# RWKV-7 branch of a hybrid decoder layer: groups of four head pairs over 256 tokens instead of two over 512

## The chip, the cores and the metric

The kernel runs on one core of a Trainium2 chip. The core has TensorE (matmuls, called PE in the profile; PEld is its weight load), VectorE (DVE), ScalarE (ACT), GpSimd (POOL) and SyncE (SP), which here only issues transfers. The metric is device time in microseconds for one execution; less is better.

## The reference, cut to what matters

One layer, 2048 tokens, model width 1024, float32. A normalised input is projected into three branches; each branch's output is gated, projected back, merged and added to the input. Branch A is the one that changes:

```
p = rms_norm(x) @ w_in                       # split into p_r, p_k, p_v, p_w, p_a, z_a, ...
r, k, v = token_shift_mix(...)               # u + (prev - u) * mu
decay = exp(-exp(-softplus(-(w0 + tanh(lw) @ w2)) - 0.5))
a = sigmoid(a0 + la @ a2)
kk = k * k_k / max(norm(k * k_k), 1e-12);  k = k * (1 + (a - 1) * k_a)
step t, per head (64 x 64 state S):
    S = S * w_t + (S @ -kk_t) kk_t*a_t  + v_t k_t ;  y_t = S @ r_t
y = group_norm(y) * lnx_g + lnx_b + sum(r * k * r_k) * v
y_a = y * silu(z_a)
```

There are eight heads of 64 channels. Branch B is sliding-window attention, branch C cross-attention into 256 memory tokens.

## The kernel before, in words

The tokens are taken in four superblocks of 512 (TB). The channels lie on the partitions, tokens on the free axis. The kernel keeps float32 accuracy by writing each operand as a rounded part and a rest (type f32r), so that a product is three matmuls of 512 columns (gemm3, L467 to L469). Weights come from DRAM block by block: a block is 128 x 1024 (a `whl` tile, eight buffers), loaded by SP (L445), and feeds twelve matmuls. In the first superblock the rounded parts are made on chip (L449, L450) and kept in DRAM.

Per superblock two streams are woven together: stream_r, the RWKV branch, and stream_f, the other branches with their merges. The recurrence is done in chunks of 64 tokens (C). The eight heads are four pairs, a pair filling 128 partitions (heads EV and OD). Stream_r works on two groups of two pairs, each over all 512 tokens, that is eight chunks (NC_):

- rwkv_prep, once a pair: projections of k, r and v with the token shift; products for decay and rate (L702 to L706, 512 columns); the norm of k (tok_stat L509 in the first superblock, spread_sums L520 and L521 later); the tiles QE, QO, AB and BK of each chunk; the Gram products of BK with QE and QO (L769, 32 matmul records for each of two heads' halves in one burst); transposes of BK (L786) and v (L801); the bonus sums (L795, L796). The second pair's four tiles take four of the eight `whl` buffers until the group's chain ends.
- rwkv_inverse, once a group: the inverse of a triangular block per chunk, on VectorE (L819 to L821), with two bursts of 32 x 32 matmuls.
- rwkv_chain, once a group: a serial loop over the eight chunks. In a step TensorE computes pw from the state (L899), VectorE copies it (W, L903), TensorE pu (L914), VectorE multiplies it by the key norms into Z (L920), TensorE the new state pS (L923), and VectorE adds to it SP, the old state times the chunk-end decay Pl, with pS itself multiplied by Pl (L924, four operations a step). SP is made on ScalarE (L912, four a step). Two more bursts for the outputs y (L879, L875) don't hold the loop up. TensorE's rows for these small float32 matmuls come in two records each.

The order of the work is not the order of the code. Every instruction is recorded, and a list scheduler (lay_out) with a duration for each kind of instruction (cost_PE, cost_DVE and so on), a rank by place in the code and the free buffers of each pool writes one fixed order for each engine; then these orders are tied down. The numbers that the streams yield weave their code order. Each queue works strictly in that order: an instruction that waits holds everything behind it on its engine, and a transfer that waits for a buffer or its data holds the transfers behind it on SP.

Of the kernel before, what the change touches and what calls it, by code (L numbers as in the profile page):

```python
# [9 lines left out]
F32 = mybir.dt.float32  # L10
# [4 lines left out]
ALU = mybir.AluOpType  # L15
# [13 lines left out]
NC_ = TB // C  # L29
# [278 lines left out]
def build(tc, A, nsb=4):  # L308
# [114 lines left out]
    smask = bp.tile([128, TB], BF16, name="smask")  # L423
# [99 lines left out]
    def half_sums(d, out, junk):  # L523

        j = chunks(junk)
        V.tensor_tensor(j, chunks(out), eye64.unsqueeze(1).to_broadcast([128, NC_, 64]), op=ALU.mult)
        V.tensor_reduce(d, j, axis=AX.X, op=ALU.add)
# [138 lines left out]
    Pt = cp.tile([128, NC_, 65], F32, name="Pt")  # L666
    G.memset(Pt, 1.0)
# [14 lines left out]

    EV, OD = slice(0, 64), slice(64, 128)
# [3 lines left out]
    def rwkv_prep(p, i, Z, dk, Nc, sb, hT, lwla, group):  # L687
        def big(name):

            if not i:  # L690
                return rp.tile([128, NC_, 128], F32, name=name)
            t = wp.tile([128, NC_, 128], F32, name="whl")
            G.memset(t[:, 0, 0:1], 0.0)
            return t

        QE, QO, AB, BK = (big(n) for n in ("QE", "QO", "AB", "BK"))
        bk = BK.rearrange("p c (s t) -> p c s t", t=C)
        kp = proj(B_K + p, hT)
        k = shift(kp, B_K + p, pcol("mu_k", p), dcol("omu_k", p), sb, "rk_")
        lh, ll = (t.rearrange("p (a c) -> p a c", a=4) for t in wblock(A["w2a2"][p], ("lora", p)))  # L700
        pw = rw_ps()
        PE.matmul(pw, lh[:, 0], lwla[0], start=True, stop=False)  # L702
        PE.matmul(pw, ll[:, 2], lwla[0], start=False, stop=True)
        pa = rw_ps()
        PE.matmul(pa, lh[:, 1], lwla[1], start=True, stop=False)
        PE.matmul(pa, ll[:, 3], lwla[1], start=False, stop=True)  # L706
        th = tmp()
        S.activation(th, pw, AF.Tanh, scale=0.5, bias=dcol("hw0", p))
        ta = tmp()
        S.activation(ta, pa, AF.Tanh, scale=0.5, bias=dcol("ha0", p))  # L710
        V.tensor_scalar(th, th, 1.0, None, op0=ALU.add)
        cum = tmp()
        V.tensor_tensor_scan(cum, smask, th, 0.0, ALU.mult, ALU.add)
        S.activation(Pt[:, :, 1:], chunks(cum), AF.Exp, scale=-DEC)
        Pl = xp.tile([128, NC_], F32, name="Pl", bufs=4)
        S.activation(Pl, Pt[:, :, C], AF.Copy)
        iP = tmp()
# [4 lines left out]
        yield 10.317  # L722
        st = rw_ps()
        if sb >= FIRST:
            sq = tmp()
            S.activation(sq, k, AF.Square, scale=pcol("k_k", p))
            spread_sums(st, ones2, sq, *(rp.tile([128, TB], F32R, name="rt", bufs=NRT) for _ in range(2)))
            half_sums(dk[:, i], st, sq)
            V.tensor_scalar(dk[:, i], dk[:, i], 1e-24, None, op0=ALU.max)
        else:  # L730
            sq = tmp()
            S.activation(sq, k, AF.Square, scale=pcol("k_k", p))
            tok_stat(sq, 2, 4, st)
            sums, own = st[:, :8].rearrange("p (a e) -> p a e", e=2), dk[:, i].rearrange("p (a o) -> p a o", o=2)
            for e, h in ((0, EV), (1, OD)):
                for o, at in ((0, EV), (1, OD)):
                    V.tensor_scalar(own[h, :, o], sums[at, :, e], 1e-24, None, op0=ALU.max)
# [3 lines left out]
        kkh = tmp()  # L741
# [3 lines left out]
        t2 = tmp()  # L745
# [3 lines left out]
        f = tmp()  # L749
# [5 lines left out]
        rpj = proj(B_R + p, hT)  # L755
        r = shift(rpj, B_R + p, pcol("mu_r", p), dcol("omu_r", p), sb, "rr_")
# [4 lines left out]
        yield 12  # L761

        two = ((QE, EV, OD), (QO, OD, EV))
        gs, ms = [], []
        for c0 in range(0, NC_, 4):
            gs.append([t.rearrange("p (c t) -> p c t", c=4) for t in ((rw_ps(), rw_ps()) if not c0 else (y_ps(), o_ps()))])
            for c in range(4):
                for (Q, h, oh), g in reversed(list(zip(two, gs[-1]))):
                    m = PE.matmul(g[:, c], BK[h, c0 + c], Q[h, c0 + c], start=True, stop=True)  # L769
                    if ms:  # L770
                        behind(m, ms[-1])
# [11 lines left out]
        for c0 in range(0, NC_, 4):  # L783
            pk = rw_ps().rearrange("p (c f) -> p c f", c=4)
            for c in range(4):
                PE.transpose(pk[:, c], BK[:, c0 + c], ident)  # L786
# [642 lines left out]
```

## Time and profile before

| | before |
|---|---|
| runs | 2232.64 us median of 3 (2232.46 to 2233.23) |
| the profiled execution, its span | 2231.6 us |
| TensorE | 2210.5 us busy, 13682 matmul records |
| VectorE | 1544.4 us busy, 3993 instructions |
| ScalarE | 920.2 us busy, 2042 instructions |
| GpSimd | 132.9 us busy |
| transfers | 433.17 MB, mean 194 GB/s |

The profiled execution's first to last instruction, 2231.6 us, is 1.0 us under the median. Busy time counts an engine as busy from the start to the end of each instruction; matmuls overlap, so the distances between their starts tell more than their durations. A group's line gives busy time and the mean duration of one, then the engine's idle time before it and what ended it.

### The profile page before, as it was taken

The numbers are of one execution on the slowest core, as the hardware profiler recorded it, in microseconds if no ns is written. First come the engines' busy times: TensorE is split into PE (matmuls) and PEld (weight loads), VectorE is DVE, ScalarE is ACT, GpSimd is POOL, SyncE is SP. The second block draws the span as 40 slices with busy tenths as digits, with TensorE's granted clock in tenths as the row PEclk, the third lists the DMA queues.
The fourth block names the chain that finished last, engine by engine and source line by source line (L and its number), as shares of the span: only waits on it lengthen the run. The fifth ranks groups of instructions, "written<-read, shape, count | busy, mean of one in ns | idle before, by whom it ended". The sixth has DMA issues, their size and how long they took to land. (4 is left out here: it accounts for less than half of the span.)

```text
span 2231.6 us, 36859 instructions
## 1 busy us (share of the span) xinstructions
PE 2210.5 (99%) x13682; PEld 1798.2 (81%) x13682; DVE 1544.4 (69%) x3993; ACT 920.2 (41%) x2042; POOL 132.9 (6%) x193
## 2 busy tenths in 40 slices
PE   8999999999999999999999999999999999999999
PEld 7888778778888778878888878877888887887887
DVE  7799699775479688943438958975245896896312
ACT  6664565445253355423215335432223434534210
POOL 1000010000000010000000001000000001000000
PEclk9999999999999999999999999999999999999999
DMA  6877556679845434446764534445675444344555
GB/s 218 293 240 258 186 183 217 224 274 351 313 163 167 143 133 158 146 169 231 243 237 143 178 125 150 144 142 199 222 254 198 162 156 156 119 151 132 201 196 189
DMA packets 149874, 433.17 MB, mean 194 GB/s; under 512 B 16704, under 2 KB 24256, under 8 KB 149696
## 3 DMA queue, kind: packets, MB, share of 16 engines
q1 hardware_dynamic: 133568, 401.45, 53.0%
q10 hardware_dynamic: 16128, 29.37, 3.9%
q8 instruction: 109, 1.79, 0.3%
q14 instruction: 69, 0.57, 0.1%
HBM read 334.81 MB, written 95.94 MB: 193 GB/s over the span
## 5 line engine op out<-in xcount | busy, mean ns | idle before, releaser
L467 PE MATMUL mm<-hH,whl 128*128 128x512 f32 x1888 | 752.4, 399 | 0.1
L469 PE MATMUL mm<-hH,whl 128*128 128x512 f32 x1888 | 750.2, 397 | 0.0
L468 PE MATMUL mm<-hL,whl 128*128 128x512 f32 x1888 | 745.3, 395 | 0.0
L469 PEld LDWEIGHTS mm<-hH,whl 128*128 128x128 f32 x1888 | 355.1, 188 | 71.8 <-issue 1.5
L467 PEld LDWEIGHTS mm<-hH,whl 128*128 128x128 f32 x1888 | 355.3, 188 | 68.7 <-DVE carry L677 0.4
L468 PEld LDWEIGHTS mm<-hL,whl 128*128 128x128 f32 x1888 | 355.3, 188 | 68.0 <-issue 0.9
L449 ACT ACTIVATE whl<-raw 128x512 fp32r<-128x512 f32 x178 | 111.3, 629 | 151.3 <-PE mm L469 95.1
L450 DVE TENSOR_TENSOR whl<-raw,whl 128x512 fp32r<-128x512 f32 x178 | 122.5, 691 | 48.2 <-ACT whl L449 45.9
L467 PE MATMUL mm<-yh,whl 128*128 128x512 f32 x384 | 151.9, 396 | 1.3 <-ACT gt L1190 0.8
L468 PE MATMUL mm<-yl,whl 128*128 128x512 f32 x384 | 151.1, 393 | 0.0
L469 PE MATMUL mm<-yh,whl 128*128 128x512 f32 x384 | 150.2, 391 | 0.0
L912 ACT ACTIVATE SP<-Z,Pl 64x64 f32<-64x64 f32 x256 | 76.4, 337 | 117.1 <-DVE Z L924 115.5
L819 DVE STREAM_SHUFFLE ibc<-Nc 128x496 f32<-128x496 f32 (+30 forms) x248 | 114.0, 473 | 0.0
L1205 DVE SCALAR_TENSOR_TENSOR g<-g,mm 128x512 f32<-128x512 f32 x32 | 21.8, 682 | 128.3 <-PE mm L469 128.3
L820 DVE TENSOR_TENSOR ibc<-ibc,Yi 128x496 f32<-128x496 f32 (+30 forms) x248 | 104.9, 423 | 4.1
L821 DVE TENSOR_TENSOR Yi<-Yi,ibc 128x496 f32<-128x496 f32 (+30 forms) x248 | 103.5, 418 | 1.2
L924 DVE SCALAR_TENSOR_TENSOR Z<-rw,Pl,SP 64x64 f32<-64x64 f32 x224 | 63.4, 283 | 40.6 <-PE rw L923 37.1
L1190 ACT ACTIVATE gt<-mm 128x512 f32<-128x512 f32 x64 | 37.9, 592 | 118.3 <-PE mm L469 118.2
L467 PEld LDWEIGHTS mm<-yh,whl 128*128 128x128 f32 x384 | 72.2, 188 | 16.9 <-ACT gt L1190 1.2
L468 PEld LDWEIGHTS mm<-yl,whl 128*128 128x128 f32 x384 | 72.2, 188 | 14.6
L1152 ACT ACTIVATE g<-g,mxs,st 128x256 f32<-128x256 f32 (+1 forms) x128 | 74.5, 584 | 22.8 <-DVE mxs L1145 22.6
L469 PEld LDWEIGHTS mm<-yh,whl 128*128 128x128 f32 x384 | 72.2, 188 | 14.4
(1847 smaller groups left out, 3804.7 us busy)
## 6 DMA issues: line engine op xcount, KB each, us to landing
whl<-k SPq DMA_DIRECT2D x486, 512.0 KB, 3.3
k<-whl SPq DMA_DIRECT2D x162, 512.0 KB, 4.3
raw<-in_w_in SPq DMA_DIRECT2D x118, 256.0 KB, 3.2
g<-in_x ACTq DMA_DIRECT2D x32, 256.0 KB, 4.9
out<-g ACTq DMA_DIRECT2D x32, 256.0 KB, 4.3
raw<-in_w_proj SPq DMA_DIRECT2D x24, 256.0 KB, 3.1
rt<-in_x ACTq DMA_DIRECT2D x24, 256.0 KB, 5.2
rt<-in_xt ACTq DMA_DIRECT2D x24, 256.0 KB, 5.5
```

Source lines behind the costliest of these rows:

```text
L449: S.activation(w[:, 0], raw, AF.Copy)
L450: V.tensor_tensor(w[:, 1], raw, w[:, 0].bitcast(F32), op=ALU.subtract)
L467: PE.matmul(out, lh, rh, start=i == 0, stop=False)
L468: PE.matmul(out, lh, rl, start=False, stop=False)
L469: PE.matmul(out, ll, rh, start=False, stop=i == n - 1)
L819: V.stream_shuffle(bc[:, :, :w], N_[:, :, s + 1:], [s] * 32)
L820: V.tensor_tensor(bc[:, :, :w], bc[:, :, :w], Y[:, :, s:s + 1].to_broadcast([128, n, w]), op=ALU.mult)
L821: V.tensor_tensor(Y[:, :, s + 1:], Y[:, :, s + 1:], bc[:, :, :w], op=ALU.add)
L912: S.activation(SP[h, i], Z[h, i, e, c], AF.Copy, scale=g[4][h, c:c + 1])
L924: upds = [V.scalar_tensor_tensor(Sst[h, g[0]] if c == NC_ - 1 else Z[h, i, e, c + 1], pS[h, i, e], g[4][h, c:c + 1], SP[h, i], op0=ALU.mul ...
L1152: S.activation(prs[b][:, i, m0:], prs[b][:, i, m0:], AF.Exp, scale=r2[:, b, i:i + 1], bias=mx[:, b, i:i + 1], accum_out=mx[:, b, 2 + i:3 + i])
L1190: S.activation(t, gp, AF.Tanh, scale=0.5)
```

## The change

A group is now all four pairs over half a superblock (TR = 256 tokens, so four chunks), and the halves follow each other. What a group holds is as large as before; the loop is four steps long with four pairs in each, where it was eight steps with two.

- Projections of k, r and v are still made once for 512 tokens, in the first half's rwkv_prep. The second half of each result (128 x 256) is stored to DRAM by SP and loaded again when the second half's rwkv_prep wants it (columns). The gate z_a is made in the second half.
- The other operations of rwkv_prep and the end of rwkv_chain work on 256 columns and run twice as often. The low-rank weights are loaded once for each half. The first superblock uses spread_sums, too.
- BK is multiplied by Pl (a new VectorE operation a pair and half, 128 x 512) after its Gram products and before its transposes. So pS comes out multiplied, and the step's update is an addition for all pairs of a head side: two VectorE operations. SP is made by two VectorE operations for all pairs, not by four ScalarE ones.
- The first two pairs' tiles come from a pool with two buffers, those of the last two pairs from four `whl` buffers. Pt has two tiles.

```diff
+TR = 256
+NC_ = TR // C
...
+    def bigs(i):
+        if i < 2:
+            return [rp.tile([128, NC_, 128], F32, name=n, bufs=2) for n in ("QE", "QO", "AB", "BK")]
+        out = []
+        for _ in range(2):
+            t = wp.tile([128, 2, NC_, 128], F32, name="whl")
...
+    def columns(what, p, half, sb, make, tile):
+        if half:
+            t = tile[:, :TR]
+            nc.sync.dma_start(t, later_half.pop((what, p)))
             return t
+        t = make(tile)
+        d = later_half[what, p] = dp.tile([128, TR], F32, name=f"{what}{sb}_{p}")
+        nc.sync.dma_start(d, t[:, TR:])
+        return t[:, :TR]
...
-        k = shift(kp, B_K + p, pcol("mu_k", p), dcol("omu_k", p), sb, "rk_")
+        k = columns("k", p, half, sb, lambda t: shift(proj(B_K + p, hT), ...), rp.tile([128, TB], F32, name="rk_"))
-        PE.matmul(pw, lh[:, 0], lwla[0], start=True, stop=False)
+        PE.matmul(pw, lh[:, 0], lwla[0][:, cut], start=True, stop=False)
...
+        V.tensor_tensor(BK, BK, Pl[:, i].unsqueeze(2).to_broadcast([128, NC_, 128]), op=ALU.mult)
+        pk = rw_ps().rearrange("p (c f) -> p c f", c=NC_)
...
-            for i, e, h, g in HH:
-                S.activation(SP[h, i], Z[h, i, e, c], AF.Copy, scale=g[4][h, c:c + 1])
+            for e, h in ((0, EV), (1, OD)):
+                V.tensor_tensor(SP[h], Z[h, :n, e, c], Pl[h, :n, c:c + 1].to_broadcast([64, n, C]), op=ALU.mult)
...
-            upds = [V.scalar_tensor_tensor(... pS[h, i, e], g[4][h, c:c + 1], SP[h, i], op0=ALU.mult, op1=ALU.add)
-                    for i, e, h, g in HH]
+            upds = [V.tensor_tensor(Sst[h, :n] if c == NC_ - 1 else Z[h, :n, e, c + 1], pS[h, :, e], SP[h], op=ALU.add)
+                    for e, h in ((0, EV), (1, OD))]
...
-            for p0 in range(0, 4, n):
+            for half in range(TB // TR):
...
+                for p in range(4):
+                    yield from rwkv_prep(p, Z, dk, Pl, Nc, sb, half, hT, lwla, group, yas)
```

The program's order around three places of the prediction. First TensorE, part of one step of the chain in the last superblock. Rows of 128x512 are other work; rw<-Z is pw, yps is y, rw<-W is pu, rw<-Z of 128x128 is pS. Before:

```order
L899 MATMUL rw<-Z,QE 64x64
L899 MATMUL rw<-Z,QO 64x64
L899 MATMUL rw<-Z,whl 64x64 x2
L879 MATMUL yps<-Z,QE 64x64
L879 MATMUL yps<-Z,QO 64x64
L879 MATMUL yps<-Z,whl 64x64 x2
L467 MATMUL mm<-hH,whl 128x512
L468 MATMUL mm<-hL,whl 128x512
L914 MATMUL rw<-W,AB 64x64 x2
L914 MATMUL rw<-W,whl 64x64 x2
L875 MATMUL yps<-Z,AB 64x64 x2
L875 MATMUL yps<-Z,whl 64x64 x2
```

The same place in the changed program (L910 is the old L899, L890 and L886 the old L879 and L875, L925 the old L914):

```order
L910 MATMUL rw<-Z,whl 64x64 x4
L890 MATMUL yps<-Z,QE 64x64
L890 MATMUL yps<-Z,QO 64x64
L890 MATMUL yps<-Z,QE 64x64
L890 MATMUL yps<-Z,QO 64x64
L890 MATMUL yps<-Z,whl 64x64 x4
L469 MATMUL mm<-hL,whl 128x512
L925 MATMUL rw<-W,AB 64x64 x4
L925 MATMUL rw<-W,whl 64x64 x4
L886 MATMUL yps<-Z,AB 64x64 x4
L886 MATMUL yps<-Z,whl 64x64 x4
L470 MATMUL mm<-hH,whl 128x512
```

Each burst has twice the matmuls of before, and one 512-column matmul stands between y and pu where there were two.

Second VectorE, the loop's operations. Before (rows of 128x512 are a merge of the other stream):

```order
L1205 SCALAR_TENSOR_TENSOR gt<-gt,mm 128x512
L1206 TENSOR_TENSOR mB<-mB,gt 128x512
L903 COPY W<-rw 128x128
L920 TENSOR_TENSOR Z<-rw,dk 64x2x64 x2
L924 SCALAR_TENSOR_TENSOR Z<-rw,Pl,SP 64x64 x4
L903 COPY W<-rw 128x128
```

And in the changed program (L914 copies W, L931 makes Z, L935 updates, L923 makes SP):

```order
L849 COPY ibc<-rw 32x512 x2
L914 COPY W<-rw 128x256
L931 TENSOR_TENSOR Z<-rw,dk 64x4x64 x2
L935 TENSOR_TENSOR Z<-rw,SP 64x4x64 x2
L923 TENSOR_TENSOR SP<-Z,Pl 64x256 x2
L914 COPY W<-rw 128x256
```

The update is two operations instead of four, and SP's two stand behind it, ahead of the next copy of W. (ibc belongs to the inverse.)

Third SP's queue while a group is prepared in the last superblock. Before, only weight blocks stand there:

```order
L445 DMA whl<-k_3789 128x1024
L445 DMA whl<-k_3797 128x1024
L445 DMA whl<-k_3804 128x1024
L445 DMA whl<-k_3938 128x1024
L445 DMA whl<-k_3946 128x1024
L445 DMA whl<-k_3953 128x1024
```

In the changed program's second half (rk_, rr_ and gt are the tiles of k, r and v; the L709 rows are loads of halves that were stored in the first half):

```order
L446 DMA whl<-k_4410 128x1024
L446 DMA whl<-k_4418 128x1024
L709 DMA rk__21038<-k_2_18710 128x256
L709 DMA rr__21185<-r_2_18822 128x256
L446 DMA whl<-k_4425 128x1024
L446 DMA whl<-k_4515 128x1024
L446 DMA whl<-k_4522 128x1024
L446 DMA whl<-k_2078 128x1024
L709 DMA gt<-v_2_18962 128x256
L446 DMA whl<-k_4685 128x1024
L446 DMA whl<-k_4693 128x1024
L709 DMA rk__21390<-k_3_19059 128x256
```

The loads of the halves stand between weight loads, in one queue.

More of the change, by code (lines that the diff above doesn't have):

```diff
@@ L720, in rwkv_prep @@
             pend.pop(0)()
[L722 to L737, printed above, removed]
+        yield 6.8 if half else 8
+        st = rw_ps()[:, :TR]
+        sq = th_()
+        S.activation(sq, k, AF.Square, scale=pcol("k_k", p))
+        spread_sums(st, ones2, sq, th_(F32R), th_(F32R))
+        half_sums(dk[:, i], st, sq)
+        V.tensor_scalar(dk[:, i], dk[:, i], 1e-24, None, op0=ALU.max)
         V.reciprocal(dk[:, i], dk[:, i])
```

158 lines of the change are left out of this document (77 added, 81 removed).

## The prediction

> **What bounds the kernel now.** I read the page's first two parts first, then the table of stretches, then the timeline of TensorE. The page of before:
>
> ```profile
> span 2231.6 us, 36859 instructions
> PE 2210.5 (99%) x13682; PEld 1798.2 (81%) x13682; DVE 1544.4 (69%) x3993; ACT 920.2 (41%) x2042; POOL 132.9 (6%) x193
> ...
> PEclk9999999999999999999999999999999999999999
> ```
>
> TensorE has something in flight for 99% of the span, at the full granted clock. That alone doesn't say that it is the limit, since durations overlap. [...] So I count in **distances between starts**. Next, busy time by stretch (after the heading's columns: PE, PEld, DVE, ACT, POOL, clock, DMA share and GB/s), for most of the first superblock and for the second and third:
>
> ```profile
> 60.00:450.00 390.00, 384.21 (x2591) 311.18 (x2590) 337.98 (x878) 220.76 (x492) 27.42 (x36) 1.00 0.66 227
> 600.00:1141.00 541.00, 540.16 (x3348) 439.39 (x3347) 361.99 (x956) 202.38 (x457) 30.84 (x43) 1.00 0.54 183
> 1141.00:1682.00 541.00, 539.26 (x3343) 438.24 (x3342) 362.66 (x957) 202.33 (x457) 30.84 (x43) 1.00 0.53 176
> ```
>
> From the second superblock on, TensorE is uncovered for 1 to 2 us in 541, so nothing makes it wait: the time is the sum of its distances. In the first one it is uncovered for 5.8 us in 390, with VectorE at 338 of 390. A change therefore pays only by what it takes out of TensorE's own sequence, and costs only if it makes TensorE wait. The timeline of one step of the RWKV chain in the last superblock (start, duration, instruction) shows what that sequence loses:
>
> ```profile
> 2041.75 0.40 PE L469 MATMUL mm<-yh,whl 128*128 128x512 f32 x1
> 2041.98 0.38 PE L923 MATMUL rw<-Z,BK 128*128 128x128 f32 x2
> 2042.20 0.39 PE L923 MATMUL rw<-Z,whl 128*128 128x128 f32 x2
> ...
> 2042.66 0.40 PE L468 MATMUL mm<-yl,whl 128*128 128x512 f32 x1
> ...
> 2044.25 0.39 PE L469 MATMUL mm<-hH,whl 128*128 128x512 f32 x1
> 2044.57 0.27 PE L899 MATMUL rw<-Z,QE 128*64 128x64 f32 x1
> ...
> 2044.85 0.22 PE L879 MATMUL yps<-Z,QE 128*64 128x64 f32 x1
> ...
> 2044.97 0.29 PE L879 MATMUL yps<-Z,whl 128*64 128x64 f32 x4
> 2045.19 0.50 PE L467 MATMUL mm<-hH,whl 128*128 128x512 f32 x1
> 2045.52 0.39 PE L468 MATMUL mm<-hL,whl 128*128 128x512 f32 x1
> 2045.75 0.40 PE L469 MATMUL mm<-hH,whl 128*128 128x512 f32 x1
> 2046.08 0.27 PE L914 MATMUL rw<-W,AB 64*64 64x64 f32 x2
> ...
> 2046.30 0.23 PE L914 MATMUL rw<-W,whl 64*64 64x64 f32 x2
> 2046.33 0.23 PE L875 MATMUL yps<-Z,whl 64*64 64x64 f32 x2
> 2046.48 0.50 PE L467 MATMUL mm<-hH,whl 128*128 128x512 f32 x1
> 2046.82 0.39 PE L468 MATMUL mm<-hL,whl 128*128 128x512 f32 x1
> ```
>
> A 512-column matmul costs 0.227 us (from 2042.66 to 2044.25 are seven, 1.59). A small burst costs its own work, and also something on the way in (2044.25 to 2044.57 instead of 0.227), on the way out (0.15 from the last row of L875, at 2046.33, to 2046.48) and at the first 512-column matmul behind it (0.34 to the next).
>
> **The change part by part.**
>
> *Chain.* 64 steps of two pairs become 32 steps of four. The 1152 matmuls stay; each burst is twice as long, and there are half as many. The fixed part of a burst, in the rows above:
> - L899 with L879: from 2044.25 to 2045.52 is 1.27, less two 512-column matmuls (0.454) is 0.816. Their own work is eight records in 0.28 (2044.57 to 2044.85) and eight at the rate of four in 0.12, 0.24. Fixed: 0.30.
> - L914 with L875: 2045.75 to 2046.82 is 1.07, less 0.454 is 0.616; own work, 14 records in 0.25, so 16 in 0.29. Fixed: 0.33.
> - L923: 2041.75 to 2042.66 is 0.91, less 0.454 is 0.456; own work, two records in 0.22, so four in 0.44. Fixed: 0.02.
>
> That is 0.65 us a step, and 32 steps fewer: **-20.6 us**.
>
> *Gram bursts* (16 of 32 records become 32 of 16). The same timeline, at one of them:
>
> ```profile
> 1913.87 0.39 PE L468 MATMUL mm<-hL,whl 128*128 128x512 f32 x1
> ...
> 1914.62 0.27 PE L769 MATMUL rw<-QO,BK 64*128 64x128 f32 x1
> ...
> 1914.73 0.27 PE L769 MATMUL rw<-QO,BK 64*128 64x128 f32 x1
> ...
> 1916.31 0.50 PE L521 MATMUL as__19335<-g,ones 128*128 128x512 f32 x1
> 1916.64 0.28 PE L1136 MATMUL as__19356<-KsH,g 128*128 128x256 f32 x1
> 1916.76 0.28 PE L1136 MATMUL as__19356<-KsL,g 128*128 128x256 f32 x1
> 1916.88 0.28 PE L1136 MATMUL as__19356<-KsH,g 128*128 128x256 f32 x1
> ```
>
> 1913.87 to 1916.64 is 2.77, less 0.454, less 32 records at two in 0.11 (1.76): fixed 0.56. Sixteen more would be +9.0. The changed order puts 22 of the 32 in front of a 512-column matmul, as all 16 were, and ten against other small work, which share a way in or out. Six at 0.56 and ten at half: 6.2; I take **+5.5**, with 3 and 9 as ends.
>
> *Halved matmuls.* The decay and rate products, the bonus sums and the norm sums are 120 matmuls of 512 columns (64, 32, 24) that become 240 of 256. The last three rows above give 0.12 for one of 256: 120 x (0.24 - 0.227) is **+1.6**. The first superblock's norm sums lose 32 small records and get 16 of 256 columns; I book nothing for it. Projections, transposes (their number and shape) and inverse stay as they are.
>
> Sum on TensorE: -20.6 + 5.5 + 1.6 = **-13.5 us**. Making it instead over the whole changed order, every neighbouring pair of instructions at the distance such a pair has in this trace, gives -18, since runs of small work of different kinds touch more often there. I take -15.
>
> *What must arrive in time.* VectorE's and ScalarE's groups:
>
> ```profile
> L912 ACT ACTIVATE SP<-Z,Pl 64x64 f32<-64x64 f32 x256 | 76.4, 337 | 117.1 <-DVE Z L924 115.5
> L924 DVE SCALAR_TENSOR_TENSOR Z<-rw,Pl,SP 64x64 f32<-64x64 f32 x224 | 63.4, 283 | 40.6 <-PE rw L923 37.1
> L920 DVE TENSOR_TENSOR Z<-rw,dk 64x128 f32<-64x128 f32 x128 | 36.9, 288 | 55.0 <-PE rw L914 46.8 <-ACT SP L912 2.5 <-issue 1.5
> L903 DVE COPY W<-rw 128x128 f32<-128x128 f32 x64 | 18.6, 291 | 41.6 <-PE rw L899 41.4
> L892 DVE TENSOR_TENSOR rt<-rt,st 128x256 f32<-128x256 f32 x32 | 12.4, 420 | 0.4
> L746 DVE SCALAR_TENSOR_TENSOR rt<-rt 128x512 f32<-128x512 f32 x16 | 10.9, 679 | 0.3
> ```
>
> ```profile
> 2046.65 0.61 DVE L920 TENSOR_TENSOR Z<-rw,dk 64x128 f32<-64x128 f32 x2 [1.03 <-PE rw L914]
> ...
> 2047.40 0.46 PE L923 MATMUL rw<-Z,BK 128*128 128x128 f32 x2
> ```
>
> The last two rows are of the step above: from L914's last record (2046.30) to VectorE's start is a handover of 0.35, and back from its end (2047.26) to L923 one of 0.14. The copy of W grows from 0.29 (128 columns) to 0.42 (L892's 256), the two multiplies of Z from 0.61 to 0.87, and four updates (1.13) become two additions (0.84). In the changed order sixteen records for y and a 512-column matmul stand between L899's burst and L914's: 0.48 + 0.15 + 0.33 = 0.96, for a need of 0.35 + 0.42 + 0.14 = 0.91. Between L914's and L923's stand sixteen for y and three of 512 columns: 0.45 + 0.15 + 0.33 + 0.23 + 0.23 = 1.39, for a need of 0.35 + 0.87 + 0.14 = 1.36. Both just suffice. SP, on ScalarE before, now stands on VectorE between the update and the next copy of W (0.84), while TensorE runs L899 for 0.5 and its way in; were it late, W would be late by the difference, up to 0.3 us.
>
> VectorE over a superblock: some 21 operations a pair are halved (2 x 0.42 for 0.68, so 0.16 each, 13 us for four pairs), keys times decay add eight of 0.68 (5.4), the chain goes from 16 x 2.00 (0.29 + 0.58 + 1.13) to 8 x 2.94 with SP (-8.5): +10, and +10 more in the first, whose norm sums take three operations of 0.42 in each of eight halves. ScalarE loses L912's 76 us, which it spent waiting for Z. Both have room from the second superblock on (VectorE 362 of 541); in the first, 338 of 390 is the narrow place. Bounds for new waits there: -4 (what is uncovered now goes away) to +20 (all of the work lands on TensorE). I take +1, since the order was written with the longer operations in it.
>
> *Halves through DRAM.* 48 stores and 48 loads of 128 KB, and 16 more loads of the low-rank weights, all on SP's queue between the weight loads. SP's waits and two rows of the transfers:
>
> ```profile
> SPq L445 <- PE mm L469: 1138.0, 379, 14.4
> ...
> whl<-k SPq DMA_DIRECT2D x486, 512.0 KB, 3.3
> ...
> km<-mk SPq DMA_DIRECT2D x16, 256.0 KB, 2.6
> ```
>
> SP spends half the span waiting for TensorE to give a weight buffer free: weights run as far ahead as the buffers let them. Four buffers, while the other four hold RWKV tiles, are four times twelve matmuls, 10.9 us; less 3.3 to landing, SP may be held some 7 us before TensorE notices. A store that waits for its shift, or a load for its single buffer, has to be held longer than that. I take 0, with 0 to +50 as ends. [...]
>
> **The rivals.**
> - *VectorE in the first superblock* (no change). Its 20 us more work land on TensorE, which already waits there: -15 + 15 to 20, so 2231 to 2237. For it: 87% busy there, and nothing else is as full. Against: the same row shows only 5.8 us lost at that load, and 52 us of VectorE idle.
> - *SP's queue* (slower). In the second half of a group, k and r have one buffer each, so a load stands before six or seven weight loads until the pair before is done with its buffer. There are two such places a pair, 32 in all; held 1.5 us too long at each, +48 us, so 2264; from 0.5 us on average the gain is gone. For it: SP waits up to 14.4 us on a buffer now. Against: 7 us of lead.
> - *Chain latency.* SP and the longer operations make TensorE wait 0.3 us three times in each of 32 steps: +29, so 2246. For it: the covers exceed the needs by 0.03 to 0.05 us alone. Against: the update is shorter by 0.29, and a step has 0.65 us less to pay.
> - *The change does more than the sum*: the -18 holds and the first superblock loses its waits, 2210.
>
> **How the numbers follow.** 2231.6 - 15 + 1 is 2217.6 for a profiled execution; the median of the runs is 2232.64, 1.0 above this execution's span, so 2218.6; with a little weight on the whole-order sum I say 2217. Chances: forecast 0.68, more than the sum 0.08, VectorE 0.11, SP's queue 0.07, chain 0.06. The forecast's own range is 2211 to 2224; to leave out no more than 2 in 10 it reaches to the VectorE rival: 2209 to 2232. A measurement of this kernel can tell about 0.2%, 4.5 us, from no change. Faster: 0.76 and a quarter of VectorE's and the chain's cases, 0.80. The same: 0.10, from those two. Slower: 0.10, SP's queue and the rest.
>
> **What would show it.** In the table of stretches, from the second superblock on a period of some 537 us instead of 541 with TensorE uncovered by 1 to 2 us; L923's line still at 0.11 between records; bursts of L899's line with sixteen records and one way out. Right on TensorE and wrong on the sum would show as idle time before L914's or L923's successors, released by VectorE. The SP rival would show as TensorE waiting for a DMA of whl. The prediction is wrong if the periods from the second superblock on do not shrink at all.

## The result, and the profile after

The changed kernel takes 2247.9 us (median of 4 runs, 2245.35 to 2250.5): the ratio to the kernel before is 1.0069, 95% interval 1.0055 to 1.0083. It is 15 us slower; 2217 was predicted, in a range of 2209 to 2232. The top of its page, in the profile's own order (span, busy time by engine, granted clock):

```profile
span 2246.0 us, 37825 instructions
...
PE 2208.1 (98%) x13786; PEld 1811.0 (81%) x13786; DVE 1586.0 (71%) x4233; ACT 923.8 (41%) x2252; POOL 154.0 (7%) x242
...
PEclk9999999999999999999999999999999999999999
```

The page alone shows little: TensorE is busy for 2 us less than before, in 14 us more. The table of stretches (us, then PE, PEld, DVE, ACT, POOL, clock, DMA share, GB/s) is the one to set against the rows of before:

```profile
60.00:450.00 390.00, 377.33 (x2311) 309.41 (x2310) 326.03 (x840) 220.22 (x526) 32.28 (x43) 0.98 0.70 238
600.00:1141.00 541.00, 536.29 (x3370) 439.38 (x3370) 374.16 (x1020) 203.62 (x511) 35.74 (x55) 1.00 0.56 191
1141.00:1682.00 541.00, 537.11 (x3369) 440.44 (x3368) 370.58 (x1014) 202.47 (x509) 35.76 (x55) 1.00 0.55 186
```

TensorE was uncovered for 0.8 and 1.7 us in the two later stretches, and now is for 4.7 and 3.9; in the first, 5.8 became 12.7. The granted clock of the first stretch fell from 1.00 to 0.98. VectorE in that first stretch is busy for 326 us, less than before (338): it isn't fuller there, though something is late.

To separate TensorE's own work from its waits, I add up, over each kernel's TensorE order, the distance that every neighbouring pair of instructions has in the trace of before when nothing is waited for (the whole-order sum of the prediction), and take it off the time that the trace shows. This own work is an estimate; it moves by a few us with the way the pairs are put into kinds. The stretches go from the start of one superblock's output matmuls to the next, the first one from TensorE's start:

| stretch | before: took | own work | beyond it | after: took | own work | beyond it |
|---|---|---|---|---|---|---|
| first | 557.5 | 536.0 | 21.6 | 569.0 | 529.9 | 39.2 |
| second | 540.9 | 538.2 | 2.7 | 542.6 | 534.1 | 8.5 |
| third | 542.1 | 538.2 | 3.9 | 542.0 | 534.1 | 7.9 |
| fourth | 541.2 | 537.8 | 3.4 | 542.8 | 534.1 | 8.7 |

By this estimate TensorE's own work is 18 us shorter. The time beyond it grew by 17.6 us in the first superblock and by 15.1 in the other three: -18 + 32.7 is the 15 us lost. It grew at two places.

**The end of every superblock.** TensorE's timeline at the end of the second one (start, duration, instruction; in brackets the idle time before it and who ended it):

```profile
1089.41 0.39 PE L470 MATMUL mm<-hH,whl 128*128 128x512 f32 x1
1091.15 0.73 PE L468 MATMUL mm<-yh,whl 128*128 128x512 f32 x2 [1.36 <-ACT yh L984]
1092.15 0.50 PE L469 MATMUL mm<-yl,whl 128*128 128x512 f32 x1 [0.27 <-DVE yl L985]
```

L468 with yh is the first matmul that projects the RWKV branch's output. It comes 35.4 us after the last burst for y; before, 85.2 us of TensorE work lay between the two (in the first superblock 36.7, and 67.1 before). The chain of waits shows what fills the time up to it:

```profile
1083.93 1.00 ACT rt L955 x2
1084.94 1.16 ACT rt L958 x3
1086.12 0.77 DVE ya L959 x2
...
1089.52 0.77 DVE ya L959 x2
1090.29 1.21 DVE ya L961 x2
1091.50 0.60 DVE yl L985
```

These are the normalisations and gate products of the last pairs. With groups of two, two pairs were finished half a superblock earlier and two came at the end; now all four come at the end, with their four z, and the RWKV stream ends later in the weave: its yields add to some 350 instead of 284, while the other stream's factor (1.42 in PACE) stayed. Before, eight gate projections, which wait for nothing of this branch, stood behind it. Now two of them are left between the last burst for y and the merge, together with the four z, and the pairs' ends come after all of these. ScalarE's last operations for the branch, the rounded parts yh, show it, before and now:

```profile
1032.79 2.67 ACT L973 ACTIVATE yh<-ya 128x512 fp32r<-128x512 f32 x4
```

```profile
1090.47 2.19 ACT L984 ACTIVATE yh<-ya 128x512 fp32r<-128x512 f32 x4
```

Before, the merge's first matmul comes at 1078.5 us, 43 us after they are done; now at 1091.15 us, while they still run. So what counts is less how much work lies behind the last burst for y than how much of it lies behind the pairs' ends.

**The second half's preparation in the first superblock.** There 19.5 us beyond TensorE's own work lie between 330 and 420 us; before, 1.7. The waits of TensorE in this stretch, the four longest (us in total, times, longest):

```profile
PE rw L796 <- DVE BK L793: 2.7, 1, 2.7
PE mm L468 <- ACT whl L450: 2.0, 1, 2.0
PE as__3900 L1147 <- DVE mxs L1151: 1.2, 1, 1.2
PE mm L468 <- ACT gt L1201: 1.2, 1, 1.2
```

They have no releaser in common: the keys times the decay (L793, an operation that is new with the change), a rounded weight (L450), the scores of the window attention (L1151), a gate (L1201). What may have changed for all of them is how much TensorE has in hand. In this stretch the first matmuls of the three-part products were L467 before, L468 now:

```profile
330.00:420.00 90.00, 40.89 (x104) 19.38 (x103) 1.00 0.69 231
```

```profile
330.00:420.00 90.00, 30.36 (x73) 14.22 (x72) 0.92 0.53 175
```

104 (before, the first row) became 73. More than half of this drop is the lost time itself: at the old rate 70.5 us of own work instead of 88.3 would leave 83 (an estimate). The rest fits what the change does: the second group brought its own projections of k, r and v, and the second half takes them from DRAM, so that less stands beside VectorE's and ScalarE's part of the preparation. That this is the cause is a supposition so far; e10 tests it.

**A wait that cost more than its length.** The third superblock's output matmuls, after one of the waits at its end:

```profile
1656.97 0.39 PE L1233 MATMUL mm<-whl,g 128*128 128x512 f32 x1
1659.16 0.50 PE L1233 MATMUL mm<-whl,g 128*128 128x512 f32 x1 [1.81 <-DVE g L1216]
...
1660.68 0.63 PE L1234 MATMUL mm<-whl,g 128*128 128x512 f32 x1
1661.10 0.63 PE L1235 MATMUL mm<-whl,mB 128*128 128x512 f32 x1
...
1663.66 0.57 PE L1235 MATMUL mm<-whl,mB 128*128 128x512 f32 x1
1664.07 0.39 PE L1233 MATMUL mm<-whl,g 128*128 128x512 f32 x1
```

After 1.8 us of idle time the granted clock is halved (0.50 between 1660.7 and 1663.9 us) for 3.4 us, and matmuls of 512 columns start 0.427 us apart instead of 0.228: eight of them, 1.6 us more. In the first superblock this happens at 336, 346 (6.8 us long), 394 and 548 us (clock 0.50 in each); before, nowhere between 16 and 2231 us (1.00). By the distances of the rows in these stretches that is, as an estimate, some 7 us in all, which the "beyond it" column holds.

### The profile page after: what moved, and what is told of

It is laid out like the page before. It is cut to its first block, busy times and chain, and to the rows that moved or that the text cites. A ratio compares the mean times of both kernels' runs of the same rounds, so it can differ in the third digit from the quotient of the medians.

```text
span 2246.0 us, 37825 instructions
## 1 busy us (share of the span) xinstructions
PE 2208.1 (98%) x13786; PEld 1811.0 (81%) x13786; DVE 1586.0 (71%) x4233; ACT 923.8 (41%) x2252; POOL 154.0 (7%) x242
## 4 chain that ended last, share of the span: by engine, by line
PE 82%; DVE 9%; ACT 4%; DMA 3%; issue 1%; POOL 1%; ACTq 0%; SPq 0%; DVEq 0%; POOLq 0%
PE mm L468 20%; PE mm L469 20%; PE mm L470 20%; PE rw L934 1%; PE mm L1235 1%; PE mm L1233 1%; PE mm L1234 1%; PE rw L780 1%; ACT g L1163 1%; PE oo L1189 1%; DMA rt<-in_x 1%; PE rw L910 1%; PE rw L925 1%; PE yps L886 1%; PE yps L890 1%
## 5 line engine op out<-in xcount | busy, mean ns | idle before, releaser
L468 PE MATMUL mm<-hH,whl 128*128 128x512 f32 x1888 | 749.3, 397 | 4.6 <-ACT whl L450 2.0
L468 PEld LDWEIGHTS mm<-hH,whl 128*128 128x128 f32 x1888 | 355.4, 188 | 75.1 <-ACT whl L450 2.7
L450 ACT ACTIVATE whl<-raw 128x512 fp32r<-128x512 f32 x178 | 111.3, 630 | 172.6 <-PE mm L470 116.6
L468 PE MATMUL mm<-yh,whl 128*128 128x512 f32 x384 | 151.5, 396 | 7.8 <-ACT yh L984 6.7
L1201 ACT ACTIVATE gt<-mm 128x512 f32<-128x512 f32 x64 | 38.0, 594 | 185.0 <-PE mm L470 167.8
L468 PEld LDWEIGHTS mm<-yh,whl 128*128 128x128 f32 x384 | 72.3, 189 | 24.8 <-ACT yh L984 8.4
L1201 ACT ACTIVATE g<-mm 128x512 f32<-128x512 f32 x32 | 19.0, 594 | 135.3 <-PE mm L470 135.2
L433 POOL TENSOR_SCALAR st<-st 128x4 f32<-128x4 f32 (+1 forms) x32 | 12.6, 394 | 864.0 <-DVE st L1012 391.8
L437 POOL TENSOR_TENSOR st<-st,mhalf 128x8 f32<-128x8 f32 (+2 forms) x40 | 56.5, 1412 | 3.3
```

Source lines behind the costliest of these rows:

```text
L437: G.tensor_tensor(out, out, mhalf[:, :n], op=ALU.pow)
L450: S.activation(w[:, 0], raw, AF.Copy)
L468: PE.matmul(out, lh, rh, start=i == 0, stop=False)
L1201: S.activation(t, gp, AF.Tanh, scale=0.5)
```

## The experiments

Times are medians; ratios are to the kernel before on the same chip. Stretches are those of the table above.

### e1: the other streams stretched

```diff
-PACE = [[[1.0] * 120, [1.42] * 120] for _ in range(2)]
+PACE = [[[1.0] * 120, [1.75] * 120], [[1.0] * 120, [1.75] * 120]]
```

> The changed kernel with one number altered: the factor on the other stream's steps in the weave, 1.42 to 1.75, so that the RWKV stream (whose steps now add up to 350 instead of 284) stands as early against the other stream as before. Theory A (the RWKV stream now ends last in each superblock and its last part has nothing left to run under): TensorE's waits from the second superblock on fall from 25 us to about 10, as before, and the time falls by about 15 us, to some 2232; with part of the first superblock's waits gone too, to 2225. Theory B (VectorE has too much to do everywhere, or the halves through DRAM hold SP up): the same waits at other places, 2243 to 2250.

Measured: 2328.4 us, ratio 1.043 (1.0415 to 1.0446). Stretches 588.6, 563.7, 563.6, 562.7. That is far outside of what either theory gave. 83 us of work now stand between the last burst for y and the RWKV merge, so the end is covered, and yet 80 us are lost on the changed kernel: TensorE now waits in the second half of every superblock's weave, where the second half's preparation meets other parts of window attention and the merges. Its timeline in the second superblock:

```profile
989.79 1.15 PE L1189 MATMUL oo<-g,Vt 128*64 128x128 f32 x18
993.87 0.73 PE L468 MATMUL mm<-yh,whl 128*128 128x512 f32 x2 [2.93 <-ACT yh L984]
...
996.85 0.79 PE L468 MATMUL mm<-hH,whl 128*128 128x512 f32 x1 [0.86 <-DVE gt L1216]
```

So a covered end isn't enough, and this factor didn't serve to cover it: it shifts everything.

### e7 and e8: the factor shifted in both directions

```diff
-PACE = [[[1.0] * 120, [1.42] * 120] for _ in range(2)]
+PACE = [[[1.0] * 120, [1.25] * 120], [[1.0] * 120, [1.5] * 120]]     # e7
+PACE = [[[1.0] * 120, [1.55] * 120], [[1.0] * 120, [1.3] * 120]]     # e8
```

> The changed kernel with the weave's factor of the other stream at 1.25 in the first superblock and 1.50 in the others (1.42 in both before; 1.75 in the run above cost 20 us in the first and 21 in each of the others). If what counts is which of the other stream's VectorE work falls on the second half's preparation, which has no projections of its own: a factor above 1.42 loses again, 545 to 552 us for each of the last three superblocks, and one below gains before the end and loses at it, 565 to 575 us for the first. If the bare end alone counts: 538 to 541 for the last three, and over 575 for the first.

> The same with 1.55 in the first superblock and 1.30 in the others. By the first reading (what falls on the second half's preparation): first superblock 575 or more, the others 541 to 546, with waits only at the end. By the bare end alone: first superblock 560 to 566, the others 546 or more, since only 44 us of TensorE's sequence are left behind the last chain burst.

Measured, one run each and so without an interval: 2284.7 and 2287.2 us. First stretch 587.5 at 1.25, 569.0 at 1.42, 582.8 at 1.55, 588.6 at 1.75 (e1); the mean of the later three 551 at 1.30, 542 at 1.42, 549 at 1.50, 563 at 1.75. Neither reading held: in each run each of them has one kind of superblock right and the other wrong. Both directions lose in both kinds of superblock: of the factors that were run, 1.42 is the best for the changed kernel. No other was run on the kernel before. What differs by tens of us between such weaves are the waits.

### e2: less VectorE work in the first superblock

The key norms of the first superblock are made as before the change (by tok_stat, with small matmuls) and no longer by three VectorE operations more a pair and half:

```diff
-        spread_sums(st, ones2, sq, th_(F32R), th_(F32R))
-        half_sums(dk[:, i], st, sq)
...
+        if sb >= FIRST:
...
+        else:
+            tok_stat(sq, 2, 2, st)
...
+            for e, h in ((0, EV), (1, OD)):
+                for o, at in ((0, EV), (1, OD)):
+                    V.tensor_scalar(own[h, :, o], sums[at, :, e], 1e-24, None, op0=ALU.max)
```

> The changed kernel, but the first superblock forms its key norms with small float32 matmuls against two columns, as before, which takes about 10 us from VectorE there. Theory A with its second part (VectorE is the narrow place of the first superblock, and waits of about 3 us there also bring stretches at half the granted clock): 5 to 10 us less, 2238 to 2243, all of it before 571 us, and fewer stretches at clock 0.5. If the first superblock's loss is a matter of the weave alone: no change, 2246 to 2250.

Measured: 2251.5 us, ratio 1.0088 (1.0072 to 1.0105), first stretch 572.4 (569.0 without the edit). Nothing is gained. The stretch from 60 to 450 us:

```profile
60.00:450.00 390.00, 375.73 (x2320) 308.76 (x2319) 325.06 (x840) 216.04 (x518) 29.82 (x43) 0.98 0.69 237
```

TensorE is uncovered for 14.3 us (12.7) at the same load of VectorE, 325 of 390. But the edit hardly relieves VectorE: over the whole span it is busy for 1584.5 us instead of 1586.0, where 10 less were expected, in part because four small operations (L757) stand in the place of one for each pair and half. So e2 says little about VectorE's load. The traces of before and after say more: up to the first output matmul VectorE is busy for 453.6 us before and 457.3 after, and between 330 and 420 us, where most of the time is lost, for 87.2 and 76.9 of 90. VectorE hasn't become fuller there.

### e3 and e4: the two halves of the change apart

e3 is the changed kernel without the decay on the keys: SP is made on ScalarE again, and the step has eight updates (two a pair) that multiply by Pl. e4 is the kernel before, groups of two over 512 tokens, with the decay on the keys and SP on VectorE.

```diff
-        V.tensor_tensor(BK, BK, Pl[:, i].unsqueeze(2).to_broadcast([128, NC_, 128]), op=ALU.mult)     # e3: gone; e4: added
...
```

> The change without the decay on the keys: groups of four pairs over 256 tokens, SP on ScalarE and eight updates with multiplication a step, as before. TensorE's sequence is the same as the changed kernel's within 1 us. VectorE loses 12 us a superblock (BK times decay, SP) and gains 11 (eight updates of 0.28 for two of 0.42), and the loop's update takes 2.3 us instead of 0.84. Theory A: within 6 us of the changed kernel, since the end of the superblock is as bare; if SP on VectorE is what makes TensorE wait: 10 us or more less.

> The kernel before with the decay on the keys alone (two pairs, 512 tokens; SP as two VectorE operations, two additions a step). TensorE's sequence is 2 us shorter by the distances of before. VectorE gets 5 us a superblock more. Theory A: 2229 to 2234, the same as before. If the decay on the keys is what costs: 2240 or more.

Measured: e3 2258.0 us, ratio 1.0112 (1.0097 to 1.0128), stretches 579.5, 542.5, 542.2, 542.2; e4 2231.6 us, ratio 0.9994 (0.9985 to 1.0004), stretches 555.4, 541.2, 541.6, 541.2. The decay on the keys alone changes nothing that can be measured; the new grouping makes the loss, 25 us alone and 15 with the decay. e3 had been expected within 6 us of the changed kernel and is 10 slower. These 10 us lie in the first superblock (579.5 against 569.0); the later stretches are alike with and without the decay. Why the decay helps there isn't shown; a shift of the weave alone can do as much (e12).

### e6: the halves stored and loaded twice

```diff
-            nc.sync.dma_start(t, later_half.pop((what, p)))
+            first, again = later_half.pop((what, p))
+            nc.sync.dma_start(t, again)
+            nc.sync.dma_start(t, first)
...
-        nc.sync.dma_start(d, t[:, TR:])
+        for d in later_half[what, p]:       # two pieces of DRAM
+            nc.sync.dma_start(d, t[:, TR:])
```

> The changed kernel with every second half of k, r and v stored to DRAM twice and loaded twice into the same tile (96 more transfers of 128 KB on SP's queue). TensorE's order is the same, instruction by instruction. SP's queue as the cause: the loss of 15 us grows by as much or more, 2260 and up. Theory A (the transfers are hidden): within 3 us of the changed kernel, 2245 to 2251.

Measured: 2247.2 us, ratio 1.0066 (1.0051 to 1.0081), that is, the changed kernel's time. 96 more transfers on SP's queue cost nothing that can be measured, which speaks against a cost of the first 96. The sign that the prediction named, TensorE waiting for a transfer of weights, comes once in the changed kernel (us in total, times, longest):

```profile
PE mm L468 <- DMA whl<-k: 0.5, 1, 0.5
```

SP's longest item of waiting is still the one on TensorE for weight buffers, 952 us (1138 before):

```profile
SPq L446 <- PE mm L470: 952.2, 344, 9.5
```

### e5: the gate projections behind the RWKV stream

The end of a superblock is to be covered without a shift of the weave. The last eight gate projections, which need nothing but the normalised input, move in the code from the other stream to the place behind both:

```diff
             yield from merge(1, *yb, accs, hT)
-            for o in range(8):
-                gates.append(gate(0, o, hT))
-                yield 5.908
...
             split_y(yas[p], *ya, "a", p, sb)
+        for o in range(8):
+            gates.append(gate(0, o, hT))
```

> The changed kernel with the other stream's last eight projections (the gates of the RWKV merge) written behind the RWKV stream's end instead of woven into it, so that TensorE has them when the last group is finished off. By the distances of the trace 75 us of TensorE's sequence then lie between the last chain burst and the first output matmul instead of 56 (before: 108). Theory A (the end of a superblock is bare): the 1.5 + 0.4 us wait at the first matmul of the RWKV merge goes, and the waits at the output shrink; 2 to 5 us less per superblock, 2230 to 2241. If the loss in the later superblocks has another cause: 2244 to 2251.

Measured: 2229.75 us, ratio 0.9987 (0.9977 to 0.9997). Stretches 566.4, 538.1, 538.2, 537.1, with 36.1, 4.0, 4.1 and 3.4 us beyond TensorE's own work. From the last burst for y to the RWKV merge there are now 52 us in the later superblocks, and the wait at it is gone:

```profile
1084.01 0.60 PE L536 MATMUL as__11898<-c_ident,rt 128*128 128x128 f32 x4
1084.36 0.48 PE L468 MATMUL mm<-yh,whl 128*128 128x512 f32 x1
```

The pairs' ends now come earlier, and the gates behind them:

```profile
1046.78 2.20 ACT L984 ACTIVATE yh<-ya 128x512 fp32r<-128x512 f32 x4
```

In the first superblock no more than 32 us lie between the last burst for y and the merge, fewer than in the change, and still nothing waits, since there, too, gates stand behind the pairs' ends. The bare end cost about 4.5 us in each later superblock. In the first one the end costs nothing any more either (0.3 us from 420 us on, 5.8 in the changed kernel), but 18.0 us stay between 330 and 420 us.

### e9: the same edit on the kernel before

> The kernel before with its last eight gate projections written behind the end of the RWKV stream, as in e5; TensorE's order stays what it was, instruction for instruction. Theory (the end of a superblock is bare only in the changed kernel, because its RWKV stream ends last): no change, 2232 +-4, stretches of 557, 541, 541, 541, and no wait over 1 us at the first matmul of the RWKV merge. Rival (writing the gates late pays in any case, through the order of VectorE and ScalarE): some 4 us a superblock here too, 2216 to 2222.

Measured: 2232.9 us, ratio 1.0 (0.999 to 1.001), stretches 556.6, 541.1, 542.2, 541.1. TensorE's order doesn't change by it at all: the planner had put the gates behind the RWKV stream by itself. So this run takes nothing away and adds nothing, and is no test of late gates on that kernel. It shows that the kernel before already had the place in the order that e5 gives back.

### e10: work for the second half's preparation

On top of e5, each pair's z (one projection, twelve matmuls of 512 columns, and its silu) is made in the second half's preparation and no longer at the chain's end:

```diff
+        if half:
+            zs[p] = silu2(B_ZA + p, hT, None)
         pb = rw_ps()[:, :TR]
...
-            z = silu2(B_ZA + p, hT) if half else None
...
-            def rest(p=p, yt=yt, yc=yc, var=var, z=z):
+            def rest(p=p, yt=yt, yc=yc, var=var, z=zs[p] if half else None):
```

> The changed kernel with the gates written last (e5: 2229.8) and, besides, each pair's z (the projection and its silu) in the second half's preparation, where only halves from DRAM come, instead of at the chain's end. TensorE then has 12 matmuls of 512 columns (2.7 us) more between each pair's transposes of the keys and its bonus sums. Theory A (the first superblock's 9 us over before are the second half's preparation running dry for want of projections): the waits of 3.4 us at L796 and the half-rate stretches at 348 and 396 us go, first stretch some 558, in all 2220 to 2223. Theory B (VectorE and ScalarE are late there through the window attention, whatever TensorE has in hand): first stretch 564 to 570, in all 2228 to 2234. Four of the eleven buffers of g are held longer; were that the limit, waits at the window attention would grow in all superblocks, 2240 or more.

Measured: 2221.3 us, ratio 0.9948 (0.9933 to 0.9963): 11 us faster than the kernel before and 27 faster than the change. Stretches 558.5, 542.3, 535.5, 535.0. The time and the first stretch came out as theory A had them, and the waits at L796 and the half-rate stretches at 348 and 396 us are gone (granted clock between 330 and 420 us: 0.94 in e5, 0.98 in e10). Its mechanism is borne out only in part, because most of the lost time went to another place of the first superblock. Between 300 and 420 us, e5 (the first row) leaves TensorE uncovered for 12.4 us and e10 for 11.0:

```profile
300.00:420.00 120.00, 107.63 (x738) 85.10 (x737) 102.77 (x278) 76.97 (x198) 15.58 (x22) 0.96 0.52 177
```

```profile
300.00:420.00 120.00, 109.02 (x758) 89.57 (x758) 102.70 (x277) 77.43 (x202) 15.13 (x22) 0.97 0.56 194
```

Beyond TensorE's own work, the change has 2.0 us between 300 and 330 us and 19.5 between 330 and 420 (e5 18.0); e10 has 12.4 and 3.1, where the 12.4 hold the wait shown below, which lies at 329.7 to 333.6 us. That is 6 us less in the sum, and not 16. The new waits are in the last steps of the first half's chain (2.1 us at L937, 1.7 at L913, both for VectorE's Z), in the window attention (1.8) and at a merge:

```profile
333.60 0.50 PE L468 MATMUL mm<-yh,whl 128*128 128x512 f32 x1 [3.90 <-ACT gt L1203]
```

The second superblock has one such wait, too (2.5 us at 1081.5 us, with a half-rate stretch: clock 0.98 between 1020 and 1100 us, 1.00 in e5). The third and fourth have none: 1.5 and 1.4 us beyond TensorE's own work, and in the third TensorE is covered throughout:

```profile
1141.00:1676.00 535.00, 535.00 (x3379) 442.26 (x3378) 374.25 (x1017) 204.52 (x509) 33.61 (x55) 1.00 0.57 189
```

### e11: the early z without the late gates

> The changed kernel with each pair's z in the second half's preparation (as in e10), but with the gates woven in as the change has them. Between the last burst for y and the first output matmul TensorE then has work for 34 us (the changed kernel 56, e5 55 to 75, e10 46 to 53). Theory (two separate causes, the dry preparation and the bare end): the second to fourth stretches keep the wait at the RWKV merge or get a longer one, 541 to 546, and the first still loses there: 2243 to 2258, so that z early pays only where the end is covered. Rival (the dry preparation was the larger cause): 2226 to 2238.

Measured: 2232.4 us, ratio 1.0001 (0.9992 to 1.0011), stretches 565.7, 540.3, 539.0, 538.5. That is in the range of the rival and better than the first theory had it, but not for the rival's reason: of the 13 us between the two profiled executions 3 lie in the first superblock and 10 in the others, where e5 had shown the loss to be at the end. The later superblocks gain 2 to 4 us each: without the four z the end of the RWKV stream is shorter, so that the merge comes 12 us after the last burst for y with waits of 0.6 and 0.2 us instead of 1.4 and 0.3. The first one loses 7.1 us at its end (e10 none) and is like e10 between 300 and 420 us. Early z alone are worth 15.5 us, late gates alone 18, both 26.6: the end is partly mended by either.

### e12: the weave's numbers following the work

On top of e10, the yield behind the chain, which stood for the four z, and the one behind the preparation:

```diff
-        yield 3.4 if half else 2.5
+        yield 5.55 if half else 2.5
...
-        yield 10.587 if half else 2
+        yield 2
```

> e10 with the numbers of the weave following the work: the pause behind the chain, which held the four z (10.587), becomes 2, and the one behind each pair's preparation 5.55 instead of 3.4. TensorE's sequence by neighbour distances is 1 us shorter. If e10's remaining losses (waits of 4.1 us at the first-half chain's neighbours at 334 us and 2.6 us at 1082 us, both at the first matmul of a merge) are coincidences of the weave: they move or vanish, 2212 to 2226. If any shift of the weave loses, as in e7 and e8: 2230 or more.

Measured: 2231.3 us, ratio 0.999 (0.9981 to 1.0). Stretches 563.8, 543.2, 536.3, 535.8. TensorE's own work is 0.9 us shorter and the time 10 us longer; the waits of the first superblock went to other places (10.9 us between 300 and 330, 10.0 between 330 and 420). So early z by themselves don't keep the time between 330 and 420 us away, and a shift of the weave is worth 10 us, as e7 and e8 said on a larger scale. The loss between 300 and 330 us isn't a coincidence of one weave: TensorE is uncovered there for 6.6, 6.4 and 9.1 us in e10, e11 and e12, the three runs with early z, and for 1.3 in the change and 1.5 in e5. e10 is the best that was run.

## Why the prediction was wrong

**TensorE's sequence: right.** The chain, Gram and halving terms were to give -13.5, the whole-order sum -18, and -15 was taken. The -18 of the table above is that same sum once more and no second measurement. What the traces show by themselves are e10's last two superblocks: TensorE is covered throughout, and the stretches are 535.5 and 535.0 us, where before took 542.1 and 541.2 with 1.3 and 1.2 uncovered. Some 537 had been forecast. The Gram and halving terms were not measured one by one. The fixed part of a burst is as it was read. TensorE in the last superblock of the changed kernel:

```profile
1915.82 0.61 PE L934 MATMUL rw<-Z,BK 128*128 128x128 f32 x4
1916.27 0.61 PE L934 MATMUL rw<-Z,whl 128*128 128x128 f32 x4
...
1917.88 0.39 PE L469 MATMUL mm<-hL,whl 128*128 128x512 f32 x1
1918.20 0.27 PE L910 MATMUL rw<-Z,QE 128*64 128x64 f32 x1
...
1918.72 0.22 PE L890 MATMUL yps<-Z,QO 128*64 128x64 f32 x1
...
1918.95 0.40 PE L890 MATMUL yps<-Z,whl 128*64 128x64 f32 x8
1919.28 0.50 PE L470 MATMUL mm<-hH,whl 128*128 128x512 f32 x1
1919.62 0.40 PE L468 MATMUL mm<-hH,whl 128*128 128x512 f32 x1
```

From 1917.88 to 1919.62 is 1.74 us; less 0.454 for two matmuls of 512 columns, less 0.52 for the first sixteen records (1918.20 to 1918.72) and 0.46 for the other sixteen (eight in 0.23, 1918.72 to 1918.95), 0.31 are left: 0.30 was predicted, and it is paid once for twice as many records. L934 has no such part, as L923 had none.

**New waits: the step that failed.** "I take +1, since the order was written with the longer operations in it", between bounds of -4 and +20 for the first superblock, and nothing for the others. It was +32.7: 17.6 in the first and 15.1 in the rest. The bound for the first superblock held, the choice of +1 within it did not. For the others no term stood in the sum, because they were uncovered for 1 to 2 us only, and I had read from this that nothing makes TensorE wait there. That row says that the old order hid every latency. It says nothing of the new order, in which the RWKV stream ends last, with four pairs to finish at once and nothing left behind them. That this bare end has its price is shown by e5: in the later superblocks the time beyond own work falls from 25.1 us to 11.5 (before: 10.0), in the first one by 5.5 us at the end. How much of it is the late end and how much the four pairs at once is not told apart. The yields that set this stood in the full diff, and the place (last burst for y to the merge, 85 us of work with the eight gates at its end) could have been read from the trace before.

**The chain's own waits: right.** The covers of 0.96 and 1.39 us sufficed. The groups of VectorE (busy, mean ns, then idle before and releaser):

```profile
L931 DVE TENSOR_TENSOR Z<-rw,dk 64x256 f32<-64x256 f32 x64 | 26.9, 421 | 30.9 <-PE rw L925 30.1
L923 DVE TENSOR_TENSOR SP<-Z,Pl 64x256 f32<-64x256 f32 x64 | 26.8, 419 | 3.5 <-ACT Pl L738 1.9
L935 DVE TENSOR_TENSOR Z<-rw,SP 64x256 f32<-64x256 f32 x48 | 20.3, 422 | 18.4 <-PE rw L934 18.0
L914 DVE COPY W<-rw 128x256 f32<-128x256 f32 x32 | 13.6, 424 | 36.4 <-PE rw L910 36.1
```

The three of the loop (L931, L935, L914) wait for TensorE and not the other way round, SP hardly waits, and their means of 0.42 us are the 0.42 that was taken. The chain-latency rival's time (2246) came out, but not its mechanism: no wait of 0.3 us stands at L925 or L934 in the later superblocks; the changed kernel has one, at L934 at 290 us.

**VectorE in the first superblock: the place, not the mechanism.** The rival gave 15 to 20 us more there, and there were 17.6. But it put them down to 20 us more work on VectorE, and up to the first output matmul VectorE is busy for 457.3 us, 453.6 before. What grew in the first superblock are the bare end (5.8 us, 0.3 in e5) and the time between 330 and 420 us (19.5, 1.7 before); elsewhere less was lost than before. The cause of the second stays open in part. That TensorE's stock of work that waits for nothing ran out there is likely and not shown: e10 adds to the stock and shortens the first stretch by 8 us against e5, but most of the waiting moves ahead, to 300 to 334 us, and e12 has the same early z and 5 us of these 8 back.

**SP's queue: nothing**, as taken. e6 doubles its transfers at no cost that can be measured, and TensorE waits 0.5 us for weights in all. **The half-rate clock** was in no step; after a wait of 1.8 us it cost 1.6 us more in the rows at 1659.16 to 1664.07.

**The forecast's sum** was -15 + 1; with the table's terms it is -18 + 32.7. What stays open: what the first superblock's waits around the second half's preparation hang on, why the best factor of those run is the one that the kernel before had, and why early z bring waits between 300 and 330 us. No run tells these apart.

## What to carry to other kernels

Where TensorE is covered all the time, a shorter sequence of its own was worth its full price here only where each stretch kept enough independent work beside its latencies. List, for each place where a serial tail or a preparation runs, how much free work stood there before, and how much will; count for a tail only what can stand behind its last operation. When a change moves where a stream ends or takes its projections away, move independent work there by hand (late gates, early z: 27 us here), and do it by moving pieces and not by a global factor, which here shifted everything else as well (+37 to +80 us). Look afterwards whether the waits are gone or only stand elsewhere.

## What was not expected of the hardware

No step of the prediction had the granted clock fall. In the changed kernel's trace it fell around short waits of TensorE, and not around all of them. Between 60 and 2200 us eleven waits last 1 us or more. With each of the four longest a stretch at half rate (0.50) begins between the start of the wait and 2.1 us after its end:

| idle, us | ended at, us | stretch at half rate begins at, us | lasts, us |
|---|---|---|---|
| 2.74 | 346.72 | 346.49 | 6.8 |
| 2.03 | 393.11 | 394.27 | 3.4 |
| 2.60 | 545.80 | 547.87 | 3.4 |
| 1.81 | 1659.16 | 1660.62 | 3.4 |

Of the seven waits of 1.16 to 1.41 us, five have none near them: three of 1.36 at the RWKV merge (to 1091.15, 1632.79 and 2176.00 us), 1.16 (to 403.84) and 1.22 (to 1120.98). One of 1.20, to 333.72 us, is followed by a stretch at 336.25 (3.4 us). The seventh, 1.41 to 547.94, comes right behind the 2.60 of the table; where waits lie as close together as that, a stretch can't be put down to one of them. In the kernel before, the only wait of 1 us or more between 20 and 2225 us, 1.17 to 254.68, has none. Why some waits have a stretch by them and others none, no run here tells.
